# Output products of two FFN chunks by seven half-size products for each pair of output tiles

## The chip, the cores and the metric

The kernel runs on one core of a Trainium2 chip. The metric is the time of one execution on the device in microseconds (us). A core has a matrix engine (TensorE, PE in the profile, with PEld for its weight loads), a vector engine (VectorE, DVE), a scalar engine (ScalarE, ACT), GpSimd (POOL) and a queue engine (SyncE, SP) that here only starts DMA transfers. Each engine works through its own queue of instructions in order and waits on semaphores for the others. Matmuls write to PSUM, which has 8 banks; everything else lies in SBUF.

## The reference

A decoder trunk of two layers over 528 tokens (16 meta tokens and 512 others) of width 1024, all in float32. Layer 0 mixes tokens by a chunked gated linear attention, layer 1 by sliding-window attention over a key/value set made once from the residual stream. Around each mixer stand two FFNs, so there are four in all:

```python
def swiglu(x, w_in, w_out):
    gate, up = jnp.split(x @ w_in, 2, axis=-1)
    return (jax.nn.silu(gate) * up) @ w_out

h = h + 0.5 * rmsnorm(swiglu(rmsnorm(h, g[0]), w_ffn_in[layer, 0], w_ffn_out[layer, 0]), g[1])
```

The inner width is 2816, that is 22 tiles of 128. The change is about `x @ w_in` (1024 by 5632) and `... @ w_out` (2816 by 1024), and mostly about the second.

## The kernel before

**Precision.** Every float32 operand of a large product is split into a rounded high part and the rest (`hi`, `lo`, both of type fp32r). ACT copies the value to `hi`, DVE forms `value - hi`. A product is then three matmuls: hi*hi, lo*hi, hi*lo. Weights are split after they land, in `split_part` (lines 226, 227) or, for the chunks below, in `split_pair` (246, 247).

**An FFN** (`ffn`, line 590 on) walks over four chunks of the 22 inner tiles: 0 to 3, 4 to 9, 10 to 15, 16 to 21 (`FF_CHUNKS`). For each chunk it makes the gated values (in products, then silu(gate)*up) and then adds their share of the output to `Y`, eight output tiles of 128 (out products). The first chunk is done plainly. For chunks two to four the in products of one inner tile go by Strassen's scheme in Winograd's form (class `Strassen`, line 709): gate and up are the two row blocks, the two halves of the tokens (264 each in layer 0, 256 in layer 1) are the two column blocks, the two halves of the 1024 inputs are the inner blocks. Seven half-size products of 4 x 3 = 12 matmuls each take the place of eight. Left factors are called 11, 12, 22 (blocks) and s1 to s4 (sums of blocks), right factors 11, 21, 22 and t1 to t4; the right ones are made once for an FFN by `right_factors` and take 14 tiles of SBUF for its whole length.

**The seven left factors of a tile** come from `load_unit` and `split_pair`: five raw pieces of 128x512 are loaded by SP, two of them get another piece added by an accumulating DMA that POOL starts (line 252), two further sums are made on DVE (262, 267), and each of the seven parts is split on ACT and DVE into a tile of its own.

**Out products** (`out_steps`, line 505) of chunks two to four are plain: for each output tile m and group of tokens, six inner tiles times three matmuls, added in one PSUM bank, then `Y += bank` on DVE (line 555). In layer 0 there are two groups (272 and 256 tokens), 288 matmuls for a chunk; in layer 1 one group of 512, 144 matmuls. The first three groups begin with the five inner tiles that are done, while the sixth is finished (`begin`).

**What orders the work.** The program is written out once, by a planner (`Flow`) that counts time on TensorE and lets small jobs (generators) put their instructions in between; `yield STEP` is a pause of 1.1 us on that clock. The build may still put an instruction whose inputs are ready ahead of others on its engine. SBUF is shared out as `SLOTS` tiles of 128x2x528 float32 (the pool `hp`), which hold split weights, factors, scratch and gated values alike, and `RAWS` raw pieces. `set_ahead(n, slots)` says how many weight parts may be asked for ahead and how many of them may hold a tile: 10 (`RING`) through chunks two to four. At most two units of seven are in the making at once (`CHAINS`).

In the Strassen class a tile's products run over `head` (11), `body` (s1, s2, 12, s3) and `tail` (s4, 22), with the head of the next tile between body and tail. Copies between them on ACT (742, 747, 749, 751) take values out of PSUM before the bank is added to again, and DVE and ACT finish gate and up (753 to 776). On the last tile of a chunk `tail` starts the first out products between s4 and 22.

Of the kernel before, what the change touches and what calls it, by code (L numbers as in the profile page):

```python
# [9 lines left out]
F32 = mybir.dt.float32  # L10
# [3 lines left out]
ALU = mybir.AluOpType  # L14
# [4 lines left out]
KD = 8  # L19
# [105 lines left out]
def trunk_kernel(ctx: ExitStack, tc, a, out):  # L125
# [53 lines left out]
    for layer in range(2):  # L179
        for f in range(2):  # L180
            for lo, hi in FF_CHUNKS:
                for t in range(lo, hi):
                    pair = [a["w_in"][layer, f, t, 0], a["w_in"][layer, f, t, 1]]
                    units += pair if lo == 0 else [pair]
                if lo < LAST:
# [50 lines left out]
    def split_pair(i, raws):  # L236


        r11, r12, r22, r1, r3 = raws
        parts, ready = loaded[i]  # L240
        (g, u), half = units[i], lambda t, c: t[:, c * 512 : (c + 1) * 512]

        def part(name, src):
            yield from slot(i)
            w = pair_tile(f"w{i}_{name}")
            act.activation(w[:, 0, :512], src, AF.Copy)  # L246
            dve.tensor_tensor(w[:, 1, :512], src, w[:, 0, :512].bitcast(F32), op=ALU.subtract)  # L247
            parts[name].append(w)
            ready[name].finish(flow)

        def onto(dst, src):
            pool.dma_start(dst, src, accum_op=ALU.add)  # L252
# [7 lines left out]
        yield STEP  # L260
        yield from part("s3", r3)
        dve.tensor_tensor(r3, r3, r22, op=ALU.add)  # L262
        yield STEP
        yield from part("s2", r3)
        yield STEP
        yield from part("12", r12)
        dve.tensor_tensor(r12, r12, r3, op=ALU.add)
        yield STEP
        yield from part("s4", r12)
        yield STEP  # L270
        yield from part("22", r22)
        chains[0] -= 1
        prefetch()

    def load_unit():
        i = len(loaded)
        asked[0] += costs[i]
        owed[i] = costs[i]
        if isinstance(units[i], list):
            g, u = units[i]  # L280
            chains[0] += 1
            raws = [raw_tile(f"raw{i}_{k}") for k in range(5)]
            for k, src, c in ((0, g, 0), (3, u, 0), (4, g, 0), (2, u, 1), (1, g, 1)):
                sp.dma_start(raws[k], src[:, c * 512 : (c + 1) * 512])
                dma_end[0] = max(dma_end[0], flow.clock) + 512 * 1.5e-3
            names = ("11", "12", "22", "s1", "s2", "s3", "s4")
            loaded.append(({k: [] for k in names}, {k: Job(None) for k in names}))
            gen = split_pair(i, raws)
        else:
            n = units[i].shape[-1]  # L290
            raws = []
            for c in range(0, n, 512):
                m = min(512, n - c)
                raws.append((raw_tile(f"raw{i}_{c}"), m))
                sp.dma_start(raws[-1][0][:, :m], units[i][:, c : c + m])
            dma_end[0] = max(dma_end[0], flow.clock) + n * 1.5e-3
            loaded.append([])
            gen = split_unit(i, raws)
        split_jobs.append(flow.spawn(gen, dma_end[0] - flow.clock))
# [296 lines left out]
    def ffn(x, groups, finish, opening=False, tail=4):  # L596
# [31 lines left out]
        for ci, (lo, hi) in enumerate(FF_CHUNKS):  # L628
# [9 lines left out]
            else:  # L638
                flow.wait(factors)
                set_ahead(16, RING)  # L640
                tiles = Strassen(z, halves)
                cur = tiles.head(new_hid())
                while cur:
                    tiles.body(cur)
                    nxt = tiles.head(new_hid()) if len(hids) < hi - lo else None
                    if nxt is None:
                        fin = (finish, KD, True) if lo >= LAST else (None, 0, False)
                        proj = out_steps(hids, groups, x.groups, False, *fin, jobs)
# [11 lines left out]
                pass  # L660

    def right_factors(x, halves, z, plain):
        for job in x.rjob:
# [41 lines left out]


    class Strassen:
        def __init__(self, z, halves):  # L710
            self.z, (self.o, self.n) = z, halves[0]
            self.a, self.c = ([ps(f"{nm}{used[0]}_{i}")[:, : self.n] for i in range(2)] for nm in "ac")
            self.d = ps(f"d{used[0]}")[:, : self.n]
            q = self.n // 4
            zz = zeros[:, :q].unsqueeze(1).to_broadcast([P, 4, q])
            mm(self.d.rearrange("p (a c) -> p a c", c=q), zeros, zz)
            self.tiles = []

        def product(self, bank, t, left, right, first):
            parts, ready = t.pair  # L720
            flow.wait(ready[left])
            w = parts[left][0]
            for k in range(4):
                wh, wl = (w[:, i, k * P : (k + 1) * P] for i in range(2))
                xh, xl = (self.z[right][k // 2][:, i, k % 2] for i in range(2))
                mm(bank, wh, xh, first and k == 0, False, not first)
                mm(bank, wl, xh, False, False, not first)
                mm(bank, wh, xl, False, k == 3, not first)
                flow.pump()
            free_slots(1)  # L730

        def head(self, hid):
            t = Job(None)
            t.pair, t.hid, i = next_pair(), hid, len(self.tiles) % 2
            self.tiles.append(t)
            t.a, t.c, t.name = self.a[i], self.c[i], used[0]
            scratch = flat(pair_tile(f"c{t.name}", F32))
            n = self.n
# [16 lines left out]
        def tail(self, t, proj):  # L755
# [14 lines left out]
            def gated():  # L770
                dve.tensor_tensor(t.g1, t.a, t.g1, op=ALU.mult)
# [3 lines left out]
                act.activation(t.hid[:, 0, g], t.h, AF.Copy, scale=-1.0)  # L775
                dve.scalar_tensor_tensor(
# [584 lines left out]
```

## Time and profile before

| | |
|---|---|
| three runs | 1899.66, 1901.35, 1901.82 us; median 1901.35 |
| the profiled execution | 1899.74 us, its span from the first to the last instruction 1897.9 us |
| mean granted TensorE clock | 0.995 |
| busy, share of the span | PE 98%, PEld 94%, DVE 71%, ACT 53%, POOL 16% |

The page gives each engine's busy time, 40 slices of the span, the DMA queues, the chain of work that ended last, the costliest groups and the DMA issues. A line such as `L162 PE MATMUL y<-hidl0f,w 128*128 128x272 f32 x144 | 19.6, 288` reads: line 162, matmuls that write tile y from hidl0f and w, 144 of them, together 19.6 us busy, 288 ns for a single one; as matmuls overlap in the pipeline, the busy time and not the 288 ns says what each adds. Line 162 is the one line that issues all matmuls, so tiles tell them apart: `y` are out products, `a`, `c`, `d`, `e` the seven products. Numbers in tile names are left out.

### The profile page before, as it was taken

The page shows a single profiled execution, that of the slowest core. Times are in us where ns is not written, and L with a number is a line of the kernel's source. Part 1 is how long each engine was busy: PE and PEld are TensorE (multiplying, and loading weights), DVE is VectorE, ACT ScalarE, POOL GpSimd, SP SyncE. Part 2 cuts the span into 40 slices and gives each one's busy share as a digit, 9 for nine tenths or more (in the row PEclk, how much of TensorE's full clock was granted, in tenths as well). Part 3 has the DMA queues.
Part 4 walks back from the last instruction along what each step waited for, and adds up shares of the span by engine and source line. Part 5 has one row for each costly group of instructions (what it writes and reads, how often), then busy time and mean ns, then how long its engine had stood idle before and what let it go on. Part 6 is the DMA issues. An engine that isn't in the chain of part 4 may idle for free.

```text
span 1897.9 us, 37052 instructions
## 1 busy us (share of the span) xinstructions
PE 1867.6 (98%) x14290; PEld 1783.6 (94%) x14290; DVE 1353.8 (71%) x2681; ACT 1005.2 (53%) x2181; POOL 304.0 (16%) x352
## 2 busy tenths in 40 slices
PE   8999999999999999999999999999999999999997
PEld 8999999999999999999999898989977897989897
DVE  6884848686574978484878775858788598858484
ACT  6662626564445666262665563636556565626363
POOL 2101010310001210101033001010353131010102
PEclk9999999999999999999999999999999999999998
DMA  5655556322113255555642456556321215565551
GB/s 192 150 153 138 152 144 167 106 68 79 45 64 105 68 133 151 139 149 142 168 154 56 104 155 153 151 150 174 106 68 34 79 47 124 158 151 156 149 146 45
DMA packets 133105, 231.19 MB, mean 122 GB/s; under 512 B 14912, under 2 KB 27584, under 8 KB 132928
## 3 DMA queue, kind: packets, MB, share of 16 engines
q1 hardware_dynamic: 111904, 190.94, 31.2%
q0 software_dynamic: 20736, 37.76, 12.7%
q8 instruction: 112, 1.84, 0.4%
q14 instruction: 65, 0.53, 0.1%
q10 hardware_dynamic: 288, 0.13, 0.0%
HBM read 226.67 MB, written 2.10 MB: 121 GB/s over the span
## 4 chain that ended last, share of the span: by engine, by line
PE 86%; DVE 9%; ACT 3%; issue 1%; DMA 0%; SPq 0%; DVEq 0%; ACTq 0%
PE y L162 30%; PE a L162 21%; PE x L162 14%; PE c L162 10%; PE d L162 5%; PE o L162 1%; DVE w L227 1%; PE e L162 1%; DVE H L433 1%; PE po L162 1%; ACT w L226 1%; PE sc L162 1%; PE ps L162 0%; DVE st_post_l1f L432 0%; PE st_go L162 0%
## 5 line engine op out<-in xcount | busy, mean ns | idle before, releaser
L252 POOL DMA_DIRECT2D raw<-in_w_in x144 | 126.0, 935 | 986.9 <-DMA raw<-in_w_in 464.5
L247 DVE TENSOR_TENSOR w_s<-raw,w_s 128x512 fp32r<-128x512 f32 x288 | 194.8, 689 | 108.4 <-ACT w_s L246 106.9
L162 PE MATMUL y<-hidl0f,w 128*128 128x256 f32 (+1 forms) x2112 | 260.9, 285 | 1.1 <-ACT hidl0f L375 1.1
L162 PEld LDWEIGHTS y<-hidl0f,w 128*128 128x128 f32 x2112 | 258.9, 188 | 1.5 <-ACT hidl0f L375 1.3
L227 DVE TENSOR_TENSOR w<-raw,w 128x512 fp32r<-128x512 f32 x378 | 242.1, 671 | 21.0 <-ACT w L226 18.9
L162 PE MATMUL y<-hidl1f,w 128*128 128x512 f32 (+1 forms) x1344 | 251.4, 347 | 2.4 <-ACT hidl1f L375 2.4
L162 PEld LDWEIGHTS y<-hidl1f,w 128*128 128x128 f32 x1344 | 213.4, 189 | 36.9 <-ACT hidl1f L375 3.1
L246 ACT ACTIVATE w_s<-raw 128x512 fp32r<-128x512 f32 x288 | 177.7, 626 | 105.7 <-DVE raw L262 67.2
L226 ACT ACTIVATE w<-raw 128x512 fp32r<-128x512 f32 x378 | 206.5, 588 | 33.8 <-PE y L162 26.6
L247 DVE TENSOR_TENSOR w<-raw,w 128x512 fp32r<-128x512 f32 x216 | 145.3, 688 | 37.8 <-ACT w L246 36.2
L162 PE MATMUL x<-x_l0m,w 128*128 128x272 f32 (+1 forms) x1200 | 157.6, 288 | 0.0
L555 DVE TENSOR_TENSOR Y<-y,Y 128x256 f32<-128x256 f32 (+2 forms) x176 | 82.2, 474 | 104.7 <-PE y L162 104.4
L246 ACT ACTIVATE w<-raw 128x512 fp32r<-128x512 f32 x216 | 130.5, 622 | 48.0 <-PE y L162 47.0
L162 PEld LDWEIGHTS x<-x_l0m,w 128*128 128x128 f32 x1200 | 149.4, 188 | 1.2
L162 PE MATMUL a<-zl0f_t,w_s 128*128 128x264 f32 x864 | 117.2, 285 | 0.0
L162 PE MATMUL a<-zl1f_t,w_s 128*128 128x256 f32 x864 | 114.3, 281 | 0.9 <-ACT c L749 0.9
L371 POOL TENSOR_TENSOR acc_post<-acc_post,sq_post 128x256 f32<-128x256 f32 (+1 forms) x72 | 61.8, 859 | 331.7 <-ACT sq_post L370 329.4
L162 PEld LDWEIGHTS a<-zl0f_t,w_s 128*128 128x128 f32 x864 | 110.0, 188 | 0.0
L162 PEld LDWEIGHTS a<-zl1f_t,w_s 128*128 128x128 f32 x864 | 107.0, 188 | 1.9 <-ACT c L749 1.7
L162 PE MATMUL x<-x_l0f,w 128*128 128x256 f32 (+1 forms) x768 | 98.4, 289 | 7.0 <-ACT w L226 5.9
L162 PEld LDWEIGHTS x<-x_l0f,w 128*128 128x128 f32 x768 | 96.2, 191 | 8.2 <-ACT w L226 5.9
L162 PE MATMUL x<-x_l1f,w 128*128 128x256 f32 (+1 forms) x576 | 92.4, 320 | 0.0
(346 smaller groups left out, 3336.7 us busy)
## 6 DMA issues: line engine op xcount, KB each, us to landing
raw<-in_w_in SPq DMA_DIRECT2D x424, 256.0 KB, 3.7
raw<-in_w_in POOLq DMA_DIRECT2D x144, 256.0 KB, 5.2
raw<-in_w_out SPq DMA_DIRECT2D x96, 256.0 KB, 3.5
raw<-in_gla_in SPq DMA_DIRECT2D x50, 256.0 KB, 3.3
raw<-in_w_last SPq DMA_DIRECT2D x48, 256.0 KB, 3.4
raw<-in_w_out SPq DMA_DIRECT2D x64, 128.0 KB, 2.9
raw<-in_gla_out SPq DMA_DIRECT2D x16, 256.0 KB, 2.9
raw<-in_w_q SPq DMA_DIRECT2D x16, 256.0 KB, 4.2
```

The costliest lines, as they stand in the source:

```text
L162: inst = pe.matmul(o, lhs, rhs, start=start, stop=stop, skip_group_check=onto)
L226: act.activation(w[:, 0, :m], raw[:, :m], AF.Copy)
L227: dve.tensor_tensor(w[:, 1, :m], raw[:, :m], w[:, 0, :m].bitcast(F32), op=ALU.subtract)
L246: act.activation(w[:, 0, :512], src, AF.Copy)
L247: dve.tensor_tensor(w[:, 1, :512], src, w[:, 0, :512].bitcast(F32), op=ALU.subtract)
L252: pool.dma_start(dst, src, accum_op=ALU.add)
L371: pool.tensor_tensor(sums[0][:, :n], sums[0][:, :n], t[:, :n], op=ALU.add)
L433: dve.tensor_tensor(h, t, h, op=ALU.add)
L555: dve.tensor_tensor(y, p[:, :n], y, op=ALU.add)
```

## The change

In chunks two and three of each FFN (eight chunks in all) the out products go by seven half-size products too. Two output tiles 2i and 2i+1 are the row blocks, the token halves the column blocks, and the six inner tiles are parted into three and three. So a product is 3 x 3 = 9 matmuls of 264 or 256 columns. The fourth chunk stays plain.

- The weights of chunks two and three are loaded as four units of seven parts (pieces of 128x384) in place of eight plain units of 768 columns. Their two later sums are made on POOL, not DVE, and in another order.
- The right factors come from a new class `Factors`. As each inner tile is done (`add`), its gated values are negated and split as block 11 (tiles 0 to 2) or 21 and 22 (tiles 3 to 5). `upper` makes t1 on POOL. `with_lower` makes t2, t3, t4: for the pairs (0,3) and (1,4) the three sums are made on POOL, for (2,5) on DVE. The scratch tiles of the six inner tiles are kept until these are made.
- `out_halves` runs the products. Three of the seven results leave PSUM through ACT copies; DVE adds two to `Y` and forms two sums, which POOL adds to or takes from `Y`.
- SBUF: 34 tiles in place of 32, 10 raw pieces in place of 11. The weight ring is 10 tiles at first, 8 from the fifth inner tile on, 7 from the sixth and through the out products.

```diff
-SLOTS = 32
-RAWS = 11
+SLOTS = 34
+RAWS = 10
 RING = 10
+NARROW = 6
...
+                if 0 < lo < LAST:
+                    wide = [a["w_out"][layer, f, m, :, lo * P : hi * P] for m in range(KD)]
+                    units += [wide[m : m + 2] for m in range(0, KD, 2)]
...
+        if n < 512:
+            pool.tensor_tensor(r1, r3, r22, op=ALU.add)
+            yield STEP
+            yield from part("12", r12)
+            yield STEP
+            yield from part("s2", r1)
+            pool.tensor_tensor(r12, r12, r1, op=ALU.add)
+            yield STEP
+            yield from part("s3", r3)
+            yield STEP
+            yield from part("s4", r12)
...
+                inner = Factors(halves) if lo < LAST else None
...
+                        if inner and len(tiles.tiles) >= 4:
+                            set_ahead(16, NARROW + 6 - len(tiles.tiles))
+                        nxt = tiles.head(inner or new_hid())
+                    elif inner:
+                        proj = out_halves(inner, halves)
...
+    class Factors:
...
+        def part(self, name, k, hi, lo, src, sign=1.0):
+            act.activation(hi, src, AF.Copy, scale=sign)
+            dve.scalar_tensor_tensor(lo, src, sign, hi.bitcast(F32), op0=ALU.mult, op1=ALU.subtract)
...
+        def add(self, t):
+            j, n = len(self.tiles), self.n
+            self.tiles.append(t)
+            if j % 2 == 0 or j > 2:
+                self.split = self.quarters(flat(pair_tile(f"b{t.name}")))
+            c = j % 2 * 2 if j < 3 else 0
+            h = self.quarters(t.scratch)
+            self.part(["11" if j < 3 else "21"], j % 3, *self.split[c : c + 2], h[1], -1.0)
+            if j > 2:
+                self.part(["22"], j % 3, *self.split[2:], h[2], -1.0)
+                self.second.append(flow.spawn(self.with_lower(j - 3)))
...
+            pool.tensor_tensor(z1, h1, h0, op=ALU.subtract)
+            yield STEP
+            self.part(["t1"], j, t.his[:, :n], t.lows[:, :n], z1)
...
+        def with_lower(self, j):
+            yield self.first[j]
+            n = self.n
+            eng = dve if j == 2 else pool
+            t = self.tiles[j]
+            z1, z2, b12, z4 = self.quarters(t.scratch)
+            _, b21, b22, _ = self.quarters(self.tiles[j + 3].scratch)
+            eng.tensor_tensor(z2, b22, z1, op=ALU.subtract)
+            eng.tensor_tensor(b12, b12, b22, op=ALU.subtract)
+            eng.tensor_tensor(z4, b21, z2, op=ALU.subtract)
+            yield STEP if j == 2 else 3 * STEP
+            three = slice(n, 4 * n)
+            self.part(["t2", "t3", "t4"], j, t.his[:, three], t.lows[:, three], t.scratch[:, three])
...
+    def out_halves(inner, halves):
+        (o, n), _ = halves
+        tiles = Strassen(inner.get, halves, 3)
+        acc = lambda m, i: Y[:, m, o + i * n : o + (i + 1) * n]
...
+        def second(t):
+            tiles.product(t.c, t, "s1", "t1", True)
+            act.activation(t.v, t.c, AF.Copy)
+
+        def corner(t):
+            tiles.product(tiles.d, t, "12", "21", False)
+            dve.tensor_tensor(acc(t.m, 0), tiles.d, acc(t.m, 0), op=ALU.add)
+
+        def sixth(t):
+            act.activation(tiles.d, t.a, AF.Copy)
+            tiles.product(t.a, t, "s2", "t2", False)
+            act.activation(t.u2, t.a, AF.Copy)
+
+        def seventh(t):
+            tiles.product(t.a, t, "s3", "t3", False)
+            dve.tensor_tensor(t.v, t.a, t.v, op=ALU.add)
+            pool.tensor_tensor(acc(t.m + 1, 1), acc(t.m + 1, 1), t.v, op=ALU.subtract)
+
+        def third(t):
+            tiles.product(t.c, t, "s4", "22", False)
+            dve.tensor_tensor(t.u2, t.c, t.u2, op=ALU.add)
+            pool.tensor_tensor(acc(t.m, 1), acc(t.m, 1), t.u2, op=ALU.add)
+
+        def fourth(t):
+            tiles.product(t.a, t, "22", "t4", False)
+            released[0] += 1
+            dve.tensor_tensor(acc(t.m + 1, 0), acc(t.m + 1, 0), t.a, op=ALU.subtract)
+
+        p = [first(0)]
+        yield
+        second(p[0])
+        p.append(first(1))
+        act.activation(tiles.d, p[0].a, AF.Copy)
+        corner(p[0])
+        second(p[1])
+        tiles.product(p[0].a, p[0], "s2", "t2", False)
...
+        for i in (1, 2, 3):
+            if i > 1:
+                sixth(p[i])
+                corner(p[i])
+                seventh(p[i])
+            if i < 3:
+                p.append(first(i + 1))
+            third(p[i])
+            if i < 3:
+                second(p[i + 1])
+            fourth(p[i])
...
+                flow.until(lambda: self.ready(right, k))
+                xh, xl = self.z(right, k)
...
+                if isinstance(t.hid, Factors):
+                    t.hid.add(t)
+                    return
```

More of the change, by code (lines that the diff above doesn't have):

```diff
@@ new lines, in out_halves, with first @@
+    def out_halves(inner, halves):
+        (o, n), _ = halves
+        tiles = Strassen(inner.get, halves, 3)
+        acc = lambda m, i: Y[:, m, o + i * n : o + (i + 1) * n]
+        room = [None]
+        def first(i):
+            t = tiles.fresh()
+            if i % 2 == 0:
+                room[0] = flat(pair_tile(f"c{t.name}", F32))
+            base = i % 2 * 2 * n
+            t.u2, t.v = (room[0][:, base + c * n : base + (c + 1) * n] for c in range(2))
+            t.m = 2 * i
+            tiles.product(t.a, t, "11", "11", True)
+            return t
+        def second(t):
[28 more added lines that the diff above has]
+        tiles.product(p[0].a, p[0], "s2", "t2", False)
+        act.activation(p[0].u2, p[0].a, AF.Copy)
+        act.activation(tiles.d, p[1].a, AF.Copy)
+        corner(p[1])
+        seventh(p[0])
+        tiles.product(p[1].a, p[1], "s2", "t2", False)
+        act.activation(p[1].u2, p[1].a, AF.Copy)
+        third(p[0])
+        fourth(p[0])
+        seventh(p[1])
+        for i in (1, 2, 3):
[9 more added lines that the diff above has]
+            fourth(p[i])
```

92 lines of the change are left out of this document (60 added, 32 removed).

## The prediction

> **What bounds the kernel now.** I read the page first: busy time, slices, chain. Then, stage by stage, busy time in windows and the chain in two windows around the first out stages of layers 0 and 1.
>
> ```profile
> span 1897.9 us, 37052 instructions
> PE 1867.6 (98%) x14290; PEld 1783.6 (94%) x14290; DVE 1353.8 (71%) x2681; ACT 1005.2 (53%) x2181; POOL 304.0 (16%) x352
> PE 86%; DVE 9%; ACT 3%; issue 1%; DMA 0%; SPq 0%; DVEq 0%; ACTq 0%
> ```
>
> TensorE is busy nearly without a gap, and 86% of the chain is matmuls. So matmuls that go away are time, as long as nothing else becomes late in their place. Here are the first two chunks in question (82 to 142 us in products, 142 to 179 out products):
>
> ```profile
> 82.00:142.00 60.00, 60.00 (x494) 60.00 (x493) 45.16 (x81) 36.19 (x79) 5.22 (x6) 1.00 0.56 154
> 142.00:179.00 37.00, 37.00 (x306) 37.00 (x305) 17.51 (x37) 9.02 (x16) 6.14 (x7) 1.00 0.67 166
> ```
>
> The columns are window, length, busy time and count of PE, PEld, DVE, ACT and POOL, then clock, DMA share and GB/s. PE is full in both, at full clock. DVE has 45 of 60 us in the in products, but only 17.5 of 37 in the out products, ACT 9: the change puts its new work where these engines are least busy.
>
> **What goes.** The chain in those windows gives back-to-back costs, first layer 0, then layer 1:
>
> ```profile
> 140.72 1.46 PE e L162 x12
> 142.18 1.88 PE y L162 x15
> 145.51 33.21 PE y L162 x273
> ...
> 1143.53 3.46 PE y L162 x15
> 1146.99 1.42 PE a L162 x12
> 1148.41 29.92 PE y L162 x129
> ```
>
> Layer 0: 288 plain matmuls take 1.88 + 33.21 = 35.09 us. The new form has 4 pairs x 7 products x 9 = 252, that is 21 groups of 12 at 1.46, or 30.66: 4.43 less. Layer 1: 144 wide ones take 3.46 + 29.92 = 33.38; 21 groups at 1.42 are 29.82: 3.56 less. Four stages of each kind: 4 x 4.43 + 4 x 3.56 = **32.0 us** less TensorE work. A matmul more for each stage clears a bank, 0.12 us, together 1.0.
>
> **What comes, for one chunk.** Prices of DVE, ACT and POOL:
>
> ```profile
> L247 DVE TENSOR_TENSOR w<-raw,w 128x512 fp32r<-128x512 f32 x14 | 9.4, 687 | 0.1
> L227 DVE TENSOR_TENSOR w<-raw,w 128x256 fp32r<-128x256 f32 x4 | 1.7, 417 | 0.0
> L776 DVE SCALAR_TENSOR_TENSOR hidl0f<-c,hidl0f 128x528 fp32r<-128x528 f32 x5 | 3.5, 708 | 3.6 <-ACT hidl0f L775 3.6
> L753 DVE TENSOR_TENSOR c<-a,c 128x264 f32<-128x264 f32 x6 | 2.6, 428 | 0.3 <-PE a L162 0.2
> ...
> L246 ACT ACTIVATE w<-raw 128x512 fp32r<-128x512 f32 x14 | 8.4, 619 | 0.0
> L226 ACT ACTIVATE w<-raw 128x256 fp32r<-128x256 f32 x5 | 2.1, 412 | 0.2 <-PE a L162 0.2
> L742 ACT ACTIVATE d<-a 128x264 f32<-128x264 f32 x6 | 2.2, 375 | 4.7 <-PE a L162 4.7
> ...
> L371 POOL TENSOR_TENSOR acc_post<-acc_post,sq_post 128x256 f32<-128x256 f32 x54 | 45.1, 835 | 159.2 <-ACT sq_post L370 157.1 <-DVE H L433 2.0
> L1003 POOL TENSOR_TENSOR sh_q<-sh_q,csq 128x512 f32<-128x512 f32 x4 | 5.6, 1398 | 10.9 <-DVE sh_q L1001 10.9
> L252 POOL DMA_DIRECT2D raw<-in_w_in x144 | 126.0, 935 | 986.9 <-DMA raw<-in_w_in 464.5
> ```
>
> - Weight splits: 8 x (512 + 256 columns) become 28 x 384. For 384 I take the middle of 256 and 512, as no row has it: DVE 0.55, ACT 0.52. DVE 28 x 0.55 - 8 x 1.10 = +6.6; ACT 28 x 0.52 - 8 x 1.03 = +6.3.
> - Factors: six splits of 528 columns (0.71 on DVE) go; twelve of 264 (0.43) and three of 792 (about 0.98 on the same slope) come, and three sums of 264 for pair (2,5): DVE 5.2 + 2.9 + 1.3 - 4.3 = +5.1, ACT about +3.4 in the same way.
> - Leaving PSUM: 16 DVE operations before and after, at nearly equal width: 0. ACT gets 4 x 3 copies at 0.38: +4.5.
> - POOL: 8 sums of 384 (about 1.12), 9 of 264 for the factors and 8 onto `Y` (about 0.85), 8 more accumulating DMAs (0.94): 9 + 14.5 + 7.5 = +31.
> - SP: 20 loads for 16, of 192 KB; with POOL's, a chunk moves 5.5 MB in place of 3.1. Over 93 us with some 15.4 MB before, that is 190 GB/s, above the 154 and 166 shown, at a share of about 0.7 (the 0.56 and 0.67 scaled up): no bound, but a loaded piece may land later.
>
> DVE then has 62.7 + 11.7 = 74 us in a chunk of 93, ACT 59, POOL 11.4 + 31 = 42. None is over. I cost these sums at nothing for themselves; their cover is TensorE's 93 us, and a stall arises only where a result is late. I looked for the places.
>
> *The switch from in to out products.* The last pair's t2 needs the last inner tile. Before, the same place looks like this:
>
> ```profile
> 240.51 1.63 PE L162 MATMUL a<-zl0f_t,w 128*128 128x264 f32 x12
> 242.18 0.43 DVE L771 TENSOR_TENSOR c<-a,c 128x264 f32<-128x264 f32 x1 [2.00 <-PE a L162]
> 242.71 0.64 ACT L775 ACTIVATE hidl0f<-c 128x528 fp32r<-128x528 f32 x1 [2.99 <-DVE c L771]
> 243.38 0.71 DVE L776 SCALAR_TENSOR_TENSOR hidl0f<-c,hidl0f 128x528 fp32r<-128x528 f32 x1 [0.77 <-ACT hidl0f L775]
> ```
>
> The product ended at 242.1, the split at 244.1: 2 us, under 5.6 us of begun groups. After: multiply, split 21 and 22, three sums, one split of 792 on ACT and one on DVE. In line, with these prices: 0.43 + 0.38 + 0.43 + 0.43 + 1.3 + 0.9 + 1.0 = 4.9 us, with three handoffs of 0.1 (DVE's end at 242.61, ACT's start at 242.71) 5.2, less where the parts that need only the earlier product go first. Cover: four products (s1, 11, 12, s1) of 9 x 0.122 = 1.1 us and two thirds of a fifth, 5.1 us. So a bare fit: from no wait (the parts that can, go first) to 2.5 us (three or four splits of 0.55 get in between). I take 0.5, nearer to none because ready parts can go first.
>
> *Copies on ACT between products.* s3 may not start before ACT has copied u2, with one product, 1.1 us, in between. Now it has 1.46 us, and even so it was late once:
>
> ```profile
> 1139.10 0.62 ACT w L226
> 1139.72 0.52 ACT w L246
> 1140.24 0.28 ACT c L749
> 1140.56 1.67 PE a L162 x12
> ```
>
> Two splits ran ahead of the copy and TensorE waited about 0.3 us. Four such copies a stage, each late by 0 to 0.4: I take 0.6 of 1.6.
>
> *Supply of weight parts.* The ring is 7 tiles at 1.1 us, so a part can be made 7 us ahead; making one takes about 1.2 us on ACT and DVE. What sits behind it shows in the DMA issues of the page (the last column is us to landing):
>
> ```profile
> raw<-in_w_in POOLq DMA_DIRECT2D x144, 256.0 KB, 5.2
> raw<-in_w_out SPq DMA_DIRECT2D x64, 128.0 KB, 2.9
> ```
>
> A load, the accumulating DMA, the split of s1, a POOL sum, a split, a POOL sum: about 3 + 5.2 + 1.2 + 1.1 + 1.2 + 1.1 = 12.8 us before the raw piece is free again, for two pairs, which last 15.5. It fits if POOL is not held up. POOL's queue now has the `Y` sums, which wait for a product, ahead of DMAs and weight sums: each such wait delays the next pair's s1.
>
> *DVE and GpSimd at the same time.* Here the trace has a price:
>
> ```profile
> 203.28 1.29 DVE L247 TENSOR_TENSOR w<-raw,w 128x512 fp32r<-128x512 f32 x2
> ...
> 962.71 3.28 DVE L227 TENSOR_TENSOR w<-raw,w 128x512 fp32r<-128x512 f32 x3
> ...
> 961.34 4.09 POOL L371 TENSOR_TENSOR acc_post<-acc_post,sq_post 128x272 f32<-128x272 f32 x3 [38.11 <-ACT sq_post L370]
> ```
>
> A DVE split costs 1.29 / 2 = 0.65 us in a row alone, and 3.28 / 3 = 1.09 beside POOL sums: 0.45 more for each sum met. Per chunk POOL gets 25 sums. Met by none: 0. Met by all, and each as long as its own 0.85 to 1.1: 23 us, which would put DVE at 97 of 93. I take one in two at 0.45, about 6 us: DVE 80 of 93. Most of it falls in the last in tile and the 31 us of out products, so parts will be late at times: 0 to 5 us a stage; I take 0.6, near zero because parts can be made up to 7 us ahead.
>
> The Trainium skill ("SBUF — State Buffer", Who interferes with whom) says that a DVE instruction with two SBUF inputs and a GpSimd instruction that reads SBUF exclude each other for the whole instruction. The trace agrees in kind (1.09 against 0.65); by that rule one sum in two would cost its whole 0.95 us, 12 us in place of 6, with DVE at 86 of 93, which leans towards the fourth case below.
>
> *Elsewhere.* 10 raw pieces for 11 act on all stages; TensorE is 98% busy, so I take 0, with -1 to +3.
>
> **Sum.** -32.0 + 1.0 + 8 x (0.5 + 0.6 + 0.6) = -17.4 against the profiled 1899.74, that is 1882.3. The median shown is 1.6 higher; against it I say **1883 us**.
>
> **The rivals.**
>
> 1. *Forecast*: small waits, 0.7 to 3 us a stage: 1876 to 1894. Chance 0.48.
> 2. *Nothing new waits*: only the 1.0 remains: 1901.35 - 31.0 = 1870. For it: in the in products the same kind of scheme keeps PE at 60.00 of 60.00. Against it: DVE, ACT and POOL all get more, with 9 matmuls as cover for 12. Chance 0.09.
> 3. *The switch eats it*: with the t2 chain at its full 2.5 us and every copy late (1.6), each stage gives back 4.1, plus 0.12: 1901.35 - 32 + 34 = 1903. For it: both chains fit only barely. Against it: both worst cases at once. I give 1894 to 1906 a chance of 0.19, split 0.06 faster, 0.08 same, 0.05 slower.
> 4. *The other side: DVE held up by POOL*. If DVE waits out each POOL sum, 97 us of work stand in a chunk of 93, and parts come late by what cannot be moved to the next in products, where DVE has 15 us free: I put it at 6 us a stage: 1901.35 - 31 + 48 = 1918. It decides from 3.9 us a stage on, where the gain is gone. For it: the rows above, and 31 us on POOL in place of 11. Against it: it takes every sum to be met, and parts made 7 us ahead to run out. Chance 0.24.
>
> Within 0.2% (3.8 us) is what a measurement cannot tell from no change. Faster 0.48 + 0.09 + 0.06 = 0.63; same 0.08; slower 0.29. For 8 in 10 the range must reach below case 2 and into case 4: 1867 to 1914.
>
> **What would show it.** In the out products PE should show 252 matmuls of 264 or 256 columns in 31 to 34 us, against 35.1 and 33.4. Right for the switch: no idle of PE before the first s2 product above 1 us. Wrong by case 3: idle of PE there, or before s3 behind an ACT copy. Wrong by case 4: weight loads of PE waiting for DVE's split of parts, those splits at a mean of 0.8 us or more, and DVE above nine tenths in the stage. Wrong for the supply: PE waiting on s1 while POOL's accumulating DMA sits behind a `Y` sum.

## The result: slower, 1970.3 us against 1901.6

The changed kernel takes 1970.33 us (median of four runs, 1969.86 to 1978.02), the kernel before 1901.59 us on the same chip: a ratio of 1.037, 95% interval 1.035 to 1.040. The prediction was 1883 us with a range to 1914. The profiled run took 1978.02 us, the longest of the four. What follows is read from its trace, so it accounts for a span 78 us longer than before (1976.2 against 1897.9), where the medians differ by 69.

The head of the page after, in the order shown for the kernel before (span, busy time, shares of the chain):

```profile
span 1976.2 us, 38672 instructions
PE 1878.5 (95%) x14586; PEld 1799.8 (91%) x14586; DVE 1515.3 (77%) x2905; ACT 1092.5 (55%) x2445; POOL 537.6 (27%) x616
PE 58%; DVE 19%; ACT 9%; issue 6%; DMA 4%; POOL 3%; DVEq 0%; POOLq 0%; ACTq 0%; SPq 0%
```

Matmuls fell from 86% of the chain to 58%. TensorE has less work, but was busy 11 us longer than before and idle 67 us more besides. DVE is still only 77% busy, so no engine beside TensorE came near its limit. Something comes late.

Busy time by stage for the first FFN (in products of chunk two, out products, in and out of chunk three, in of chunk four; columns as in the prediction):

```profile
82.17:146.54 64.37, 62.46 (x495) 61.86 (x494) 50.32 (x81) 36.36 (x81) 16.93 (x20) 0.97 0.61 138
146.54:185.97 39.43, 34.25 (x268) 32.81 (x267) 28.93 (x54) 17.76 (x42) 19.94 (x22) 1.00 0.66 165
185.97:255.19 69.22, 63.84 (x496) 63.18 (x495) 54.46 (x88) 38.07 (x85) 20.05 (x24) 0.95 0.63 146
255.19:294.17 38.98, 34.34 (x268) 32.78 (x267) 28.34 (x54) 17.63 (x42) 19.50 (x22) 1.00 0.66 166
294.17:356.00 61.83, 60.70 (x495) 60.27 (x494) 49.53 (x87) 39.36 (x85) 8.05 (x10) 1.00 0.71 184
```

The out products, which were to get shorter, take 39 us in place of 36.6. The larger loss is in the in products, which the change hardly touches: 64.4 and 69.2 us, where the kernel before needs 60.1. Summed over all four FFNs, the in products of chunks two to four went from 713.1 to 768.8 us and the out products of chunks two and three from 285.3 to 306.0. That is 76.4 of the 78.3 us by which the span grew. The rest of the kernel hardly moved.

In two places of the stages above the clock column is below 1. After some waits TensorE runs at half clock for a while; the first window here holds such a wait, the second what follows it:

```profile
234.80:239.20 4.40, 0.15 (x2) 0.06 (x1) 2.89 (x5) 2.57 (x6) 1.79 (x2) 0.88 0.54 97
238.20:245.00 6.80, 5.86 (x26) 5.86 (x27) 4.80 (x9) 3.26 (x9) 0.09 (x1) 0.50 0.35 102
```

The mean granted clock is 0.988 in place of 0.995, which costs about 0.012 x 1976 - 0.005 x 1898 = 14 us, an estimate. So 78 us come about as -31 of matmuls, +67 of waits, +14 of clock; the other 28 lie in matmuls that last longer. Some 12 of these belong to the waits too: the trace has 94 breaks of TensorE over 0.04 us in place of 20, and the last matmul before a break shows its whole 0.29 us in place of the 0.12 that it adds in a row (an estimate, 74 x 0.17). The rest I could not divide further.

What became slower on DVE, by tile and shape (count, busy time, mean ns). First the kernel after:

```profile
L702 DVE SCALAR_TENSOR_TENSOR b<-c,b 128x264 fp32r<-128x264 f32 x36 | 34.8, 984 | 6.6 <-ACT b L701 6.1
L253 DVE TENSOR_TENSOR w_s<-raw,w_s 128x384 fp32r<-128x384 f32 x128 | 92.9, 739 | 38.7 <-ACT w_s L252 38.5
L935 DVE TENSOR_TENSOR c<-a,c 128x264 f32<-128x264 f32 x36 | 15.4, 428 | 0.7
```

Then the kernel of an experiment below that has all these sums on DVE and none on GpSimd:

```profile
L702 DVE SCALAR_TENSOR_TENSOR b<-c,b 128x264 fp32r<-128x264 f32 x36 | 15.1, 429 | 0.3
L253 DVE TENSOR_TENSOR w_s<-raw,w_s 128x384 fp32r<-128x384 f32 x128 | 69.7, 553 | 9.7 <-ACT w_s L252 9.0
```

The split of a factor takes 984 ns where it needs 429, the split of a weight part 739 where it needs 553. The sum of the same width that takes one input from PSUM (`c<-a,c`) takes 428 ns, as in the kernel before. None of this appears as a wait: what these instructions lose is counted as busy time.

### The profile page after: what moved, and what is told of

Its sections match the earlier page's. It is cut to its first block, busy times and chain, and to the rows that moved or that the text cites. A ratio compares the mean times of both kernels' runs of the same rounds, so it can differ in the third digit from the quotient of the medians.

```text
span 1976.2 us, 38672 instructions
## 1 busy us (share of the span) xinstructions
PE 1878.5 (95%) x14586; PEld 1799.8 (91%) x14586; DVE 1515.3 (77%) x2905; ACT 1092.5 (55%) x2445; POOL 537.6 (27%) x616
## 4 chain that ended last, share of the span: by engine, by line
PE 58%; DVE 19%; ACT 9%; issue 6%; DMA 4%; POOL 3%; DVEq 0%; POOLq 0%; ACTq 0%; SPq 0%
PE y L163 15%; PE a L163 15%; PE x L163 14%; PE c L163 6%; PE d L163 3%; DVE w_s L253 3%; ACT w_s L252 3%; DVE w L253 2%; DMA raw<-in_w_in 2%; ACT w L252 2%; DMA raw<-in_w_out 2%; PE o L163 1%; DVE w L231 1%; DVE raw L285 1%; DVE raw L280 1%
## 5 line engine op out<-in xcount | busy, mean ns | idle before, releaser
L253 DVE TENSOR_TENSOR w_s<-raw,w_s 128x512 fp32r<-128x512 f32 (+1 forms) x416 | 298.7, 731 | 135.9 <-ACT w_s L252 134.5
L252 ACT ACTIVATE w_s<-raw 128x512 fp32r<-128x512 f32 (+1 forms) x416 | 240.8, 592 | 154.1 <-DVE raw L280 80.9
L253 DVE TENSOR_TENSOR w<-raw,w 128x512 fp32r<-128x512 f32 (+1 forms) x312 | 216.2, 712 | 13.8 <-ACT w L252 12.1
L252 ACT ACTIVATE w<-raw 128x512 fp32r<-128x512 f32 (+1 forms) x312 | 175.6, 587 | 12.3 <-POOL Y L778 6.3
L231 DVE TENSOR_TENSOR w<-raw,w 128x512 fp32r<-128x512 f32 x250 | 173.7, 732 | 4.3 <-ACT w L230 2.9
L230 ACT ACTIVATE w<-raw 128x512 fp32r<-128x512 f32 x250 | 141.8, 620 | 0.0
L163 PE MATMUL a<-zl0f_t,w_s 128*128 128x264 f32 x864 | 122.7, 292 | 16.6 <-ACT c L913 12.5
L163 PE MATMUL y<-hidl0f,w 128*128 128x272 f32 (+1 forms) x960 | 119.0, 285 | 1.1 <-ACT hidl0f L394 1.1
L163 PEld LDWEIGHTS y<-hidl0f,w 128*128 128x128 f32 x960 | 117.8, 188 | 1.4 <-ACT hidl0f L394 1.3
L163 PE MATMUL y<-hidl1f,w 128*128 128x256 f32 (+1 forms) x768 | 114.8, 310 | 2.4 <-ACT hidl1f L394 2.4
L163 PEld LDWEIGHTS y<-hidl1f,w 128*128 128x128 f32 x768 | 104.4, 188 | 11.8 <-ACT hidl1f L394 3.1
L163 PE MATMUL a<-th,w_s 128*128 128x264 f32 (+1 forms) x384 | 78.7, 293 | 20.7 <-ACT c L768 12.9
```

Source lines behind the costliest of these rows:

```text
L163: inst = pe.matmul(o, lhs, rhs, start=start, stop=stop, skip_group_check=onto)
L230: act.activation(w[:, 0, :m], raw[:, :m], AF.Copy)
L231: dve.tensor_tensor(w[:, 1, :m], raw[:, :m], w[:, 0, :m].bitcast(F32), op=ALU.subtract)
L252: act.activation(w[:, 0, :n], src, AF.Copy)
L253: dve.tensor_tensor(w[:, 1, :n], src, w[:, 0, :n].bitcast(F32), op=ALU.subtract)
```

## The experiments

All times are medians. I began with a story from the chain of waits and tested it; it did not hold as the main cause.

**First theory: queues.** Before the first long wait of TensorE in the in products (1.91 us at 129.65), the chain reads (start, us, what):

```profile
119.72 4.68 DMA raw<-in_w_out
...
125.53 1.09 POOL c L733
126.62 0.23 POOL c L734
...
128.22 0.80 POOL c L735
...
129.05 0.03 ACT th L701
129.08 0.74 issue
129.82 0.37 ACT c L911
130.19 1.03 ACT w L252 x2
131.23 0.29 ACT c L913
131.52 0.04 issue
131.56 4.47 PE a L163 x22
```

GpSimd stands in its queue at an accumulating DMA whose target isn't loaded yet. The factor sums L733 to L735 come behind it, ACT's split `th` waits for the last of them, and behind that split stands the copy into u2 (L913) that TensorE needs. So I first moved the sums from GpSimd to DVE, group by group.

*Factor sums on DVE* (`upper` and `with_lower`):

```diff
-            pool.tensor_tensor(z1, h1, h0, op=ALU.subtract)
+            dve.tensor_tensor(z1, h1, h0, op=ALU.subtract)
-            eng = dve if j == 2 else pool
+            eng = dve
...
-            yield STEP if j == 2 else 3 * STEP
+            yield STEP
```

> The sums for the right factors (t1, and t2 to t4 of the first two pairs) on DVE in place of POOL; all else as in the changed kernel. Theory A (POOL's queue: these sums stand behind accumulating DMAs that wait for their weight pieces, ACT's split of t2 to t4 waits for the sums and holds the copy of u2 behind it, TensorE waits for that copy and then runs at half clock for 3.4 or 6.8 us): the waits of TensorE for the u2 copy in the in products (1.9 to 4.3 us at the sixth inner tile) go, with the half-clock stretches behind them; 1970 falls by 30 to 45 us, to 1925 to 1940. Theory B (DVE and POOL exclude each other at SBUF, so that DVE's splits are slow): 9 of 25 sums leave POOL and load DVE instead; a gain of at most 10 us, 1960 to 1970.

Measured 1934.28 us (ratio to before 1.018, 1.015 to 1.021): 36 us back. The in products of chunk two are at 60.3 us again.

*Weight sums on DVE* (lines 267 and 272, `pool` to `dve`):

> The two sums of 384 columns for each unit of output weights on DVE in place of POOL. Theory A: the waits in the out products for weight parts (about 2.7 us a stage, behind POOL's sums) shrink, those in the in products for the u2 copy stay: 1970 falls by 5 to 15, to 1955 to 1965. Theory B: the largest POOL sums no longer meet DVE's splits: 1950 or less, and DVE's splits of 512 columns come nearer to 0.69 us.

Measured 1964.85 us (1.034, 1.031 to 1.037).

*Sums onto `Y` on DVE* (lines 773 and 778, `pool` to `dve`):

> The sums onto Y on DVE in place of POOL. Theory A: they are not in the chain, so the same within 5 us (1965 to 1975). Theory B: a third of POOL's sums no longer meets DVE's splits: 10 to 20 us less.

Measured 1963.29 us (1.033, 1.030 to 1.036).

*All three on DVE:*

> All three kinds of sums on DVE, POOL has only accumulating DMAs in these stages, as before the change. Theory A: the gains of the two experiments on factor sums and weight sums together, less some lateness of a fuller DVE: 1910 to 1935. Theory B: no meeting of DVE and POOL at all, so nearly the whole expected gain: below 1900.

Measured 1919.71 us (1.010, 1.007 to 1.013): 51 us back, and DVE, with 200 instructions more, is busy 13 us less than in the changed kernel:

```profile
PE 1854.7 (97%) x14586; PEld 1787.9 (93%) x14586; DVE 1502.0 (78%) x3105; ACT 1093.8 (57%) x2445; POOL 359.1 (19%) x416
```

Three of the four times lie where theory A (the queue) had put them, and the third is 2 us under its range; theory B (DVE and GpSimd exclude each other) missed all four (its last range, below 1900, was reached only with 12 raw buffers, further down). But B's sizes did not allow for how unequal the sums are. The time that DVE loses falls from 92 to 40 us when the 72 factor sums go, to 74 without the 64 weight sums and to 86 without the 64 sums onto `Y` (table below): 0.7, 0.3 and 0.1 us a sum. So these four runs alone do not tell the theories apart.

That DVE is less busy with more to do is a first sign that GpSimd's queue isn't the whole story. Two edits tried the queue itself, with the sums left on GpSimd.

*The split `th` planned later:*

```diff
-            yield STEP if j == 2 else 3 * STEP
+            yield STEP if j == 2 else 12.0
```

> As the changed kernel, with the factor sums on POOL, but the planner puts the split of t2 to t4 for the first two pairs 12 us behind their sums in place of 3.3. If the harm comes from this split standing in ACT's queue ahead of the u2 copy while its sums are late (theory A), the waits for the u2 copy in the in products go although the sums stay on POOL and are no earlier: 1930 to 1945, like the kernel with these sums on DVE (1934). If the harm comes from POOL's sums themselves (their time, or their meeting DVE), nothing changes: 1960 to 1975.

Measured 1974.39 us (1.039, 1.036 to 1.042). In the trace the split still runs on ACT ahead of the copy (238.65 and 240.73 us), so this says nothing on the question.

*The split `th` tied behind the copy into u2* (for inner tiles 0 and 1):

```diff
+            if j < 2:
+                job = self.copied.setdefault(j + 4, Job(None))
+                yield job
+                behind = job.ins
...
+            if behind is not None:
+                after(behind, ins)
```

> The sums stay on GpSimd. Only the order on ACT is changed: the split of the factors t2 to t4 of inner tiles 0 and 1 stands behind the next copy of a product into u2 (L913 in the changed kernel), where it stood ahead of it. Theory (a split that waits for GpSimd's sums holds the copy behind it in ACT's queue, so TensorE waits some 4 us, 27 us in all, and then runs at half clock): most of what moving these sums to DVE gave comes here too, 1932 to 1945 us, and the waits for L913 fall below 8 us. Rival (moving the sums to DVE helped because GpSimd's queue, with the weights' accumulating DMAs in it, was relieved): within 8 us of the changed kernel, 1962 to 1978 us.

Measured 1964.93 us (1.034, 1.032 to 1.036): 5 us, where the theory said 25 to 38. The waits for the copy into u2 in the in products went from 27.2 to 17.2 us, not below 8, and all waits of TensorE from 80 to 72. ACT's order is a small part.

*No accumulating DMA for the 384-wide units*, sums still on GpSimd:

```diff
-        onto(r1, half(u, 1))
-        onto(r3, half(u, 0))
+        if n < 512:
+            dve.tensor_tensor(r3, r3, r1, op=ALU.add)
+            dve.tensor_tensor(r1, r1, r22, op=ALU.add)
+        else:
+            onto(r1, half(u, 1))
+            onto(r3, half(u, 0))
...
-        yield ADDED
+        yield STEP if n < 512 else ADDED
```

> The changed kernel, all sums on GpSimd, with the accumulating DMAs of the 384-wide units replaced by two sums on DVE each, so that no sum on GpSimd stands behind a DMA that waits for a weight of these units. If the place in GpSimd's queue is what makes the sums late (b), the waits for the copy into u2 in the in products fall by half or more and the time is 1935 to 1950 us. If it is DVE held up or the sums' own length (a, c), 1958 to 1985 us, since DVE gets 64 more sums.

Measured 1968.68 us (1.036, 1.035 to 1.038), 1.7 us less than the change. The factor sums no longer stand behind the DMAs of these units, and in all it helps nothing. But this is the sum of two effects: the in products take 22 us less (the waits for the copy into u2 fall to 16.6 us, not by half), and the out products, where DVE has 64 more sums to make, take 16 us more. So the place in the queue has a part in the in products, of a size that this run doesn't settle; 1935 to 1950 us, as for a main cause, it did not give. The same edit beside the factor sums on DVE:

> Factor sums on DVE, and for output weights no accumulating DMA: DVE makes the two sums that the DMA made (two more DVE operations of 384 columns a unit); weight sums and Y sums stay on POOL. Theory A': what is left of the loss in the out products is the time from load over accumulating DMA and POOL sum to the split. Then the waits for weight parts in the out products (9.9 us in all with factor sums on DVE) go: 1934 falls to 1915 to 1925. If they come from the POOL sums or from the next in unit alone: 1930 to 1940.

Measured 1938.15 us, 4 us worse than without it.

**Second theory: raw weights come late.** With all sums on DVE, a wait of a new kind was left in the out products. ACT, over time (start, us, and in brackets what ended its idle time):

```profile
271.28 0.63 ACT L252 ACTIVATE w_s<-raw 128x512 fp32r<-128x512 f32 x1 [3.90 <-DMA raw<-in_w_in]
273.61 0.63 ACT L252 ACTIVATE w_s<-raw 128x512 fp32r<-128x512 f32 x1 [1.70 <-DMA raw<-in_w_in]
274.14 0.37 ACT L768 ACTIVATE c<-a 128x264 f32<-128x264 f32 x1
```

ACT holds the split for the next in unit until the accumulating DMA has landed, and the copy that s3 needs stands behind it. More raw buffers would start that load sooner.

*All sums on DVE, 12 raw buffers:*

```diff
-SLOTS = 34
-RAWS = 10
+SLOTS = 33
+RAWS = 12
-NARROW = 6
+NARROW = 5
```

> All sums on DVE, 12 raw pieces in place of 10, paid for with one tile less (33) and one weight part less ahead in the out products. If the late next unit comes from too few raw pieces, its wait (2 to 4.6 us a stage) shrinks and the half-clock stretches behind it go: 1900 to 1912. If the pieces are not what it waits for: 1915 to 1925, or more for the shorter ring.

Measured 1892.22 us (0.9956, 0.994 to 0.997): faster than both kernels, and 8 us under the lower of the two ranges expected.

*All sums on DVE, 10 raw buffers, no accumulating DMA for the 384-wide units:*

> All sums on DVE and no accumulating DMA for output weights. With all sums on DVE (1920) the largest wait left in each stage stands before s3 of the last pair: ACT holds the split of s1 of the next in unit, whose accumulating DMA lands late. If it is late because raw pieces come free late, doing without the DMA for output weights frees pieces earlier and the wait shrinks: 1895 to 1910. If it is late because of the DMA of the next unit alone: 1915 to 1925.

Measured 1897.25 us (0.999, 0.998 to 1.000). The wait for the copy that s3 needs, 22.6 us in all with 10 raw buffers, is gone with 12, and 12.0 us without the DMAs. *Both together:*

> All sums on DVE, 12 raw buffers, and the accumulating DMAs of the 384-wide units replaced by two sums on DVE. With 10 raw buffers taking these DMAs away gave 22 us, with them kept 12 raw buffers gave 27 us. If both cure the same wait (a raw buffer that comes late), they don't add: 1888 to 1896 us, within 4 us of 12 raw buffers alone. If they cure different waits, 1875 to 1886 us.

Measured 1901.62 us (1.000, 0.9995 to 1.001), worse than the 12 raw buffers alone and outside both expectations: the out products of layer 0 came down to 32.4 us, but in layer 1 two of them went up to 36 and 38. Why there, stays open.

So late raw weights explain the difference from 1920 to 1892. Do they explain the change?

*12 raw buffers, all sums on GpSimd:*

> The changed kernel with 12 raw buffers in place of 10 (33 slots in place of 34, and one unit fewer ahead), all sums on GpSimd. If the supply of raw weights alone was what the change got wrong, it gains as much here as it did with the sums on DVE (27 us) or more: 1935 to 1945 us. If GpSimd's queue and ACT's held copies are first, the raws wait for the same sums and it gains under 12 us: 1958 to 1975 us.

Measured 1967.08 us (1.036, 1.034 to 1.038): 3 us, where the same buffers gave 27 with the sums on DVE.

*The same with the split `th` behind the copy:*

> Both of the two former edits together, all sums still on GpSimd. If the two causes (held copies, late raw weights) are separate and GpSimd's sums are harmless otherwise, the two gains add: some 1910 to 1925 us. If GpSimd's queue itself is late for the weights, it stays above 1930 us.

Measured 1966.83 us (1.035, 1.034 to 1.037). Order and buffers give little as long as the sums run on GpSimd.

**Third theory: GpSimd's sums hold DVE up.** The trace after already shows it, beside the chain quoted above. Two stretches over time, GpSimd and DVE together:

```profile
125.53 1.09 POOL L733 TENSOR_TENSOR c<-c,c 128x264 f32<-128x264 f32 x1
125.76 1.86 DVE L702 SCALAR_TENSOR_TENSOR b<-c,b 128x264 fp32r<-128x264 f32 x1
...
126.25 1.07 POOL L734 TENSOR_TENSOR c<-c,c 128x264 f32<-128x264 f32 x1
```

```profile
127.54 1.77 DVE L702 SCALAR_TENSOR_TENSOR b<-c,b 128x264 fp32r<-128x264 f32 x1
...
127.95 1.06 POOL L735 TENSOR_TENSOR c<-c,c 128x264 f32<-128x264 f32 x1
...
129.24 0.68 DVE L253 TENSOR_TENSOR w_s<-raw,w_s 128x512 fp32r<-128x512 f32 x1
```

A split of 0.43 us starts at 125.76, while GpSimd's sum runs, and ends at 127.62, 0.30 us after the second of two sums (127.32). The next ends at 129.31, 0.30 after GpSimd's third (129.01). By the profile this one starts 0.41 us before the sum behind which it ends; why, stays open. All that DVE had to do stood behind the two for 3.5 us. The Trainium skill ("SBUF — State Buffer", Who interferes with whom) says that a DVE instruction with two inputs in SBUF contends with a GpSimd instruction that reads SBUF, not with one that only writes, and that the one that is blocked is blocked for the whole instruction. The rows agree on the block, and on `c<-a,c` at 428 ns, which has one input in SBUF.

To part this from the queue and from the sums' own length, four kernels with all sums on DVE and 11 raw buffers. The control:

> The control of the next two: all 200 sums on DVE, 11 raw buffers, 33 slots. Between the 1920 us of 10 raw buffers and the 1892 us of 12: 1893 to 1906 us.

Measured 1905.42 us (1.002, 1.001 to 1.003). Its engines:

```profile
PE 1853.5 (97%) x14586; PEld 1784.6 (94%) x14586; DVE 1503.0 (79%) x3105; ACT 1095.2 (58%) x2445; POOL 359.1 (19%) x416
```

*Beside each of the 200 sums on DVE, one of the same width on GpSimd, on a buffer of its own that nobody reads:*

```diff
+    def beside(ins0, m):
+        ins = pool.tensor_tensor(idle[:, :m], idle[:, :m], idle[:, :m], op=ALU.add)
+        after(ins0, ins)
...
-            dve.tensor_tensor(r1, r3, r22, op=ALU.add)
+            beside(dve.tensor_tensor(r1, r3, r22, op=ALU.add), n)
```

> The control with, beside each of the 200 sums on DVE, a sum of the same width on GpSimd (in the same place of its queue) whose result nobody uses. No instruction of the others waits for it. Theory (a, GpSimd's sums hold up DVE's instructions beside them, about 0.5 us each, and the splits that come late by it hold TensorE): 20 to 45 us over the control, and the split b of 264 columns takes 0.7 us or more in place of 0.43. Theory (b, GpSimd's queue delays the accumulating DMAs): as much over the control as in the run with instructions that read nothing. Theory (c, the sums come too late for those who wait for them): within 5 us of the control.

Measured 1992.01 us (1.049, 1.046 to 1.052): 87 us over the control, twice the upper end of what I expected, for sums that no instruction of another engine waits for. Its engines, one group of its idle sums, and the split b:

```profile
PE 1882.0 (95%) x14586; PEld 1801.2 (91%) x14586; DVE 1604.5 (81%) x3105; ACT 1096.4 (55%) x2445; POOL 521.7 (26%) x617
```

```profile
L177 POOL TENSOR_TENSOR idle<-idle 128x384 f32<-128x384 f32 x64 | 67.4, 1053 | 3.5
L177 POOL TENSOR_TENSOR idle<-idle 128x264 f32<-128x264 f32 x68 | 64.8, 953 | 2.2
L177 POOL TENSOR_TENSOR idle<-idle 128x256 f32<-128x256 f32 x68 | 63.4, 932 | 1.9
```

```profile
L708 DVE SCALAR_TENSOR_TENSOR b<-c,b 128x264 fp32r<-128x264 f32 x36 | 21.7, 613 | 0.3
```

With the same instructions DVE is busy 101.5 us longer: 0.51 us for each of the 200 sums, which take 0.98 us themselves. The split b is at 613 ns, less than the 700 expected, since here the sums on DVE are held up as well.

The waits of TensorE for the copy into u2 in the in products (total in us, times, longest), first in the changed kernel, then here:

```profile
PE a L163 <- ACT c L913: 27.2, 19, 4.2
PE a L165 <- ACT c L925: 23.3, 20, 2.5
```

The control has none of 0.2 us or more. Here it is back, though no split on ACT waits for a sum on GpSimd: a DVE that is held up is enough to make it.

*Two fills of 512 columns in the same places instead* (`pool.memset(idle, 0.0)`):

> The control with two fills of a 512-column buffer on GpSimd (0.52 us each in the kernel before) in the places where the last run has a sum: GpSimd's queue is held as long, but nothing is read. Theory (a): within 6 us of the control, and the split b stays at 0.43 us. Theory (b): 15 us or more over it.

Measured 1907.21 us (1.004, 1.002 to 1.005), 1.8 us over the control. GpSimd's queue is held even longer, and DVE isn't touched:

```profile
L178 POOL MEMSET idle<- 128x512 f32 x400 | 257.1, 643 | 16.6
```

```profile
PE 1854.8 (97%) x14586; PEld 1785.6 (94%) x14586; DVE 1503.5 (79%) x3105; ACT 1095.4 (57%) x2445; POOL 571.2 (30%) x817
```

So a busy queue of GpSimd costs next to nothing here, and reading costs much.

*Copies, one input, in the same places:*

> The control (all sums on DVE, 11 raw buffers, 1905 us) with a copy on GpSimd, one input, of the same width in the place of each of the 200 sums that nobody uses. If any read of GpSimd holds DVE up, DVE's busy time rises above the control's 1503 us by about half of what GpSimd spends on the copies, 30 us or more, and the time is 1915 us or more. If it takes two inputs, DVE's busy time stays within 5 us of 1503 and the time within 8 us of the control.

Measured 1926.34 us (1.014, 1.013 to 1.016), 21 us over the control. DVE is busy 38.9 us longer, a quarter and not half of the copies' 159 us. This fits the first case expected in its time and by its 30 us or more, not in the share:

```profile
PE 1860.5 (97%) x14586; PEld 1785.4 (93%) x14586; DVE 1541.9 (80%) x3105; ACT 1097.2 (57%) x2445; POOL 479.9 (25%) x617
```

The idle sums show that hold-up alone can cost as much as the change lost. They don't show how the loss of the change divides: with the idle sums DVE makes its own 200 too and is 81% busy in place of 77%, while in the change ACT's splits also wait for sums that take about 1 us on GpSimd in place of 0.43 on DVE, and that stand behind DMAs. No run parts these two from the hold-up.

**The best version once more**, with the ring in the out products at 7 tiles as in the change (`NARROW = 6`):

> All sums on DVE, 12 raw buffers, 33 slots, and the ring of weights in the out products at 7 tiles again in place of 6. If the ring is short there, 1886 to 1891 us; if slots are short (the factors wait for them), 1893 to 1900 us.

Measured 1891.86 us (0.996, 0.994 to 0.998), the same as with 6.

The runs that carry the reading side by side (time DVE lost: summed durations of its instructions less those that the same instructions take in the kernel with all sums on DVE and as many raw buffers; waits of TensorE: gaps over 0.04 us, summed):

| sums on GpSimd | raw buffers | DVE lost, us | TensorE waits, us | time, us |
|---|---|---|---|---|
| 200, the change | 10 | 92 | 80 | 1970.3 |
| 136 (weight sums on DVE) | 10 | 74 | 77 | 1964.9 |
| 136 (`Y` sums on DVE) | 10 | 86 | 69 | 1963.3 |
| 128 (factor sums on DVE) | 10 | 40 | 49 | 1934.3 |
| none | 10 | 0 | 44 | 1919.7 |
| none | 11 | 0 | 32 | 1905.4 |
| none, 200 idle ones | 11 | 105 | 90 | 1992.0 |
| none, 200 idle copies | 11 | 42 | 43 | 1926.3 |
| none, 400 fills | 11 | 1 | 33 | 1907.2 |
| none | 12 | 0 | 22 | 1892.2 |

## Why the prediction was wrong

Most of **the matmul saving** (-32 us, +1) is there, where nothing waits. The windows of the best version's first out stage, the in stage behind it and the next out stage:

```profile
142.20:175.36 33.16, 33.16 (x268) 32.64 (x267) 30.15 (x68) 17.85 (x43) 6.14 (x7) 1.00 0.74 187
175.36:237.62 62.26, 60.96 (x496) 60.32 (x495) 51.67 (x99) 38.15 (x85) 10.99 (x13) 1.00 0.71 168
237.62:270.71 33.09, 33.09 (x268) 32.54 (x267) 30.13 (x68) 17.84 (x43) 6.51 (x8) 1.00 0.73 186
```

An out stage of layer 0 takes 33.1 in place of 36.6: 3.5 of the 4.43 counted, and 4.2 in the run where these stages took 32.4 us. All eight stages together gain 22 us. The in products give 15 us back, about 1.8 us in each that follows an out stage. One us of it is a wait for the first split of the next unit; for the rest I have no cause.

**The added work** was right. Without what it lost, DVE's instructions sum to 12.1 us more a chunk (11.7 predicted), and POOL got 29 us a chunk (31).

**DVE and GpSimd at the same time** is the step that failed. It took one sum in two to be met, 6 us a chunk; DVE lost 11.4 us a chunk, 92 us over 200 sums or 0.46 a sum. That this mean is the price of 0.45 for a sum met is partly luck: the single sums differ widely (0.7 us for a factor sum, 0.1 for one onto `Y`). And of the 6 us it put only 0.6 a stage on the path, "near zero because parts can be made up to 7 us ahead". But part of the lost time comes in blocks, as the 3.5 us for two splits above, at the moment when factors, sums for gate and up and weight parts all want DVE. Taking the sums off GpSimd gives back 51 us with 10 raw buffers and 75 with 12 (1967.1 to 1892.2), that is 6.3 and 9.4 us a chunk; idle sums cost 87, 10.8 a chunk. So the fourth rival had the mechanism, and its 6 us a stage was near the first of these; its 1918 us had nothing for the late raw weights (27 us), and its chance of 0.24 was too low. What was to show it held only in part: TensorE did wait for DVE's splits of weight parts (7.6 us in all), and the splits `w_s` of 384 columns took 0.84 us in the first out stage, though those of `w` took 0.55; but DVE stayed at three quarters of the out stage, not above nine tenths. An engine need not be full to be late.

**The place.** The prediction looked for late parts in the out products. More than two thirds of the loss (55.7 of 76.4 us) is in the in products, where all nine factor sums of GpSimd for a chunk run and TensorE waits 27 us for ACT's copies into u2. The sum had no term for that place.

**Copies between products**: TensorE waits 12.9 us for the copy that s3 needs in the out products, 1.6 a stage, the far end of the 0 to 1.6 given, against 0.6 taken. With 12 raw buffers and no sums on GpSimd it is gone, so ACT's load by itself wasn't the reason. With 10 raw buffers and no sums on GpSimd it is 22.6 us, behind late raw weights.

**The switch** waits about 0.9 us a stage, against 0.5 taken, though not before s2 as expected: the 7.2 us are for the factor 21. **Supply** was said to fit "if POOL is not held up"; the runs with 12 raw buffers show that it comes second: 3 us with the sums on GpSimd, 27 without. **Elsewhere**, 10 raw buffers cost little, as said: 1.9 us of the 78 lie outside these stages. **The clock** had no term: about 14 us.

From 1883 to 1970 are 87 us. Undone in this order, the sums on GpSimd make 51 of them and the raw weights 27, and 9 stay; with the buffers first, they make 3 and the sums 75.

**Beating both**: undoing only the move of the sums to GpSimd and giving two more raw buffers for a slot yields 1892 us. The idea of the change was sound for 8 us of the 17 predicted.

## What to carry to other kernels

Before moving element-wise work from DVE to GpSimd, compare what it takes off DVE with what it holds up there: here 93 us of sums left DVE and 92 us came back as longer instructions. Such a hold-up was in no list of waits here; look for the same instruction at two different means, and for DVE instructions that end just after one on GpSimd. And when a fix of a wait in the chain gives little (order, buffers), test the suspected engine with work that nobody waits for and with work of the same length that touches nothing.

## What the runs showed of the hardware

- A sum on GpSimd with both inputs in SBUF costs DVE half of its own time here (101.5 us for 195.6 us), a one-input copy a quarter (38.9 for 159.4), a fill nothing (0.5 for 257).
- One DVE instruction can be held over two GpSimd sums in a row (1.86 us for 0.43): DVE did not get in between them.
- TensorE falls to half clock for 3.41 or 6.83 us after some waits of about 2 to 4 us: the 1.91 us wait at 129.65 is followed by half clock from 132.35 for 3.41 us, the one of 4.25 us at 234.89 by half clock from 238.17 for 6.83 us. Not after all: the wait of 2.68 us at 871.4 in the same run is followed by none. The Trainium skill ("TensorE: Matmul & The Clock Gate", What's actually happening) has half clock after an idle window of about 3.4 us. The lengths of the stretches agree with one or two such windows; the 1.91 us wait does not, since a wait shorter than a window was enough.
